# Retention's chunks in two groups, state tiles in pairs, and a table of later steps, in a one-layer hybrid decoder kernel

## The chip, the cores and the metric

The kernel runs on one core of a Trainium2 chip. The metric is the device time of one execution in microseconds (us); lower is better. The engines are TensorE (PE), VectorE (DVE), ScalarE (ACT), GpSimd (POOL) and SyncE (SP, which here only issues DMAs).

## The reference

One layer is computed for 520 tokens: a prompt of 512 and 8 single tokens of a decode step, width 1024, all in float32. The layer is a first half-step feed-forward, a token mixer of retention and gated delta rule side by side, and a second half-step feed-forward, each between two RMS norms.

```python
def layer(x, pos, s_ret, s_gdn, s_conv, ...):
    x = x + 0.5 * rmsnorm(swiglu(rmsnorm(x, ffn1_pre_g), ...), ffn1_post_g)
    m, s_ret_new, s_gdn_new, s_conv_new = token_mixer(rmsnorm(x, mix_pre_g), pos, ...)
    x = x + rmsnorm(m, mix_post_g)
    x = x + 0.5 * rmsnorm(swiglu(rmsnorm(x, ffn2_pre_g), ...), ffn2_post_g)

def step(s, inp):            # retention, one chunk
    q_, k_, v_, G_ = inp
    o = jnp.exp(G_)[..., None] * jnp.einsum('bhid,bhde->bhie', q_, s)
    gl = G_[..., -1:]
    s = jnp.exp(gl)[..., None] * s + jnp.einsum('bhjd,bhje->bhde', k_ * jnp.exp(gl - G_)[..., None], v_)
    return s, o              # plus (q k^T * decay) v inside the chunk
```

Retention and gated delta have 4 heads each, with states of 128 x 128; the decode tokens carry 8 states per head in from memory and the new states are outputs.

## The kernel before

The 520 tokens are two halves of 260 columns. A product in float32 is made as three passes: each weight tile is split into a rounded part whi (ACT, line 318) and the remainder wlo (DVE, line 319), each activation tile into a pair likewise (xhl, lines 477 and 478), and lines 380, 381 and 382 multiply high by high, low by high and high by low. These 128 x 128 by 260-column matmuls are "the stream"; the program has 8892 of them in a fixed order: first feed-forward (gate and up products g and u, some of them as seven products sv in place of eight, then down products dn), the mixer's input projections p, the branch products br and the output product, then the second feed-forward. Weights come by DMA from SP's queue (raw, line 246) and POOL's (line 266).

All other work is side work. It is written as Python generators ("tasks"), which `spawn` puts on a list. After about every six matmuls of the stream the program calls `tick`, which advances each task that is due; a task that yields n is due again n ticks later. So the order in which the instructions stand on each engine is fixed when the program is written, and each engine takes its own in that order. `spawn` looks up a table LATER by the task's name and how often it was spawned: at entry 0 its start is moved by so many ticks, at entry k the k-th yield that is not zero is made longer (or, with a negative number, shorter). Before the change, LATER is empty.

The side work that matters here:

- The norms ahead of a part (`pre_rms`): ACT squares the eight tiles of x by halves (line 495, sq), DVE adds them up in seven additions (line 509), PE sums over partitions with a matmul by ones (line 443, ss, one column per token group), DVE makes ms (line 433), POOL takes the reciprocal root rs (line 437), and PE spreads it over the partitions (line 449, rb). ACT and DVE copy rb out of PSUM (lines 531 and 529); products made before then are multiplied by it late. The norms behind a part (`post`) do the same with sums acc that DVE gathers (line 489).
- The gated delta heads (`gdn_head`): causal convolution (cv), its transposes (tr, line 1127), gates (gc and gbc, lines 1184 and 1206), sums of squares gsq summed by cs (line 1568), and an inverse in small blocks that travel through memory on SP's queue (lines 1480 and 1483).
- The retention heads (`ret_head`): for each of four chunks of 128 tokens PE writes the output (po, lines 1303 and 1304) and the chunk's addition to the state (line 1305) into one bank, DVE brings the state st forward (lines 1311 and 1307), ACT copies the output out (line 1312), DVE takes its mean and variance (lines 1314 and 1315).
- The decode states (`state_products`): eight tiles sd of four states each per kind, loaded by SP (line 1612) one ahead of its use; PE multiplies four states by 1 or 2 columns each (sp, line 1625), DVE copies the result out (line 1626).

Of the functions that are called but not changed, `tick` is this:

```python
    def tick(self):
        self.now += 1
        self.add_sums()
        self.prefetch()
        for t in list(self.tasks):
            if t[0] <= self.now:
                ...
                    steps = next(t[1])
                    if steps:
                        t[3] += 1
                        steps += t[2].get(t[3], 0)
                    t[0] = self.now + max(steps, 1)
```

Of the kernel before, what the change touches and what calls it, by code (L numbers as in the profile page):

```python
# [15 lines left out]
P = 128  # L16
# [24 lines left out]
SLOTS = 68  # L41
PLAIN = {1: 3, 2: 4}
# [3 lines left out]
LATER = {  # L46
}
# [82 lines left out]
class Kernel:  # L130
# [368 lines left out]
    def pre_rms(self, xs, r, plus):  # L499

        nc = self.nc
        self.sq = sq = [self.slot("sq") for _ in range(KD)]
        for hf in range(2):
            for k in range(KD):
                while len(xs[hf]) <= k:
                    yield 0
                self.square(k, hf, nc.scalar)
        for k in range(1, KD):
            nc.vector.tensor_tensor(sq[0], sq[0], sq[k], ALU.add)
        while not self.leads:  # L510
            yield 0
        yield 1
        yield from self.inverse_rms(sq[0], r, plus)
# [761 lines left out]
    def ret_head(self, h, q, k, v):  # L1275
# [23 lines left out]
        mv = self.const("mv", [P, NCH, 2])  # L1299
        for i in range(NCH):  # L1300
            po = self.bank("po")
            if i:
                nc.tensor.matmul(po[:, 0:P], qg[:, i, :], st[:, i - 1, :], start=True, stop=False)
            nc.tensor.matmul(po[:, 0:P], sT[:, i, :], vt[:, i, :], start=i == 0, stop=True)
            nc.tensor.matmul(po[:, P : 2 * P], kd[:, i, :], vt[:, i, :], start=True, stop=True)
            if i:
                nc.vector.scalar_tensor_tensor(
                    out=st[:, i, :], in0=st[:, i - 1, :], scalar=float(gamma**P), in1=po[:, P : 2 * P], op0=ALU.mult, op1=ALU.add
                )
            else:  # L1310
                nc.vector.tensor_copy(st[:, 0, :], po[:, P : 2 * P])
            nc.scalar.copy(po_sb[:, i, :], po[:, 0:P])
            bs = self.small("bs", [P, 6])
            nc.vector.bn_stats(bs, po[:, 0:P])
            nc.vector.bn_aggr(mv[:, i, :], bs)
            yield 3
# [298 lines left out]
    def state_products(self, src, rhs, n):  # L1615
# [3 lines left out]
        nxt = self.load_state(src, 0)  # L1619
        yield 10  # L1620
        for i in range(8):
            s, nxt = nxt, self.load_state(src, i + 1) if i < 7 else None
            ps = self.bank("sp")
            for b in range(4):
                nc.tensor.matmul(ps[:, b * n : (b + 1) * n], s[:, b, :], rhs(i // 2, 4 * (i % 2) + b), start=True, stop=True)
            nc.vector.tensor_copy(acc[:, i * 4 * n : (i + 1) * 4 * n], ps[:, 0 : 4 * n])
            yield 7
# [205 lines left out]
```

## Time and profile before

| what | value |
|---|---|
| median of 3 runs | 1244.01 us |
| lowest and highest | 1237.38 and 1244.2 us |
| the profiled execution | 1238.32 us, of which the span from first to last instruction is 1236.6 us |
| TensorE busy | 1197.2 us, 97% of the span |
| VectorE, ScalarE, GpSimd busy | 902.7, 576.2, 280.5 us |
| mean granted TensorE clock | 0.985 of full |

All durations below come from the one profiled execution. Busy time of PE counts the modelled ends of matmuls that overlap, so it says when PE had work, not that it ran at its peak; what was lost is read from idle time and from the granted clock. A releaser is inferred from the last semaphore event, and may name a neighbour of the true one.

### The profile page before, as it was taken

What the parts mean: (1) busy time and instruction counts of PE and PEld (TensorE: products, weight loads), DVE (VectorE), ACT (ScalarE), POOL (GpSimd) and SP (SyncE); (2) the same over time, 40 slices, a digit from 0 to 9 for tenths busy, and PEclk for the clock granted to TensorE, in tenths of its full rate; (3) what the DMA queues carried; (4) which work ended last, traced back from release to release, by engine and by line L of the source; (5) the groups of instructions that cost most, each with busy time, mean ns of one, the idle gap of its engine ahead of it and who ended that gap; (6) DMA issues with size and microseconds to landing.
All of it is one profiled execution on the core that took longest, in us unless ns stands there. A gap on an engine that the chain in (4) does not pass through costs nothing.

```text
span 1236.6 us, 25500 instructions
## 1 busy us (share of the span) xinstructions
PE 1197.2 (97%) x9921; PEld 1184.5 (96%) x9921; DVE 902.7 (73%) x1940; ACT 576.2 (47%) x1209; POOL 280.5 (23%) x501
## 2 busy tenths in 40 slices
PE   8999999999998999989999999999999999999995
PEld 8999999999997999989999999999999999999995
DVE  8988888676547788667666765546888888867554
ACT  6655666454334564312333243334565666653330
POOL 4211211000014248544443111212411111000003
PEclk9999999999998999999999999999999999999997
DMA  6787776223352433332343554442587777332352
GB/s 196 207 203 196 181 179 154 63 80 94 96 174 78 132 104 110 99 108 74 111 143 115 184 187 150 136 156 69 151 252 182 181 185 184 96 92 79 95 166 69
DMA packets 79689, 170.38 MB, mean 138 GB/s; under 512 B 17232, under 2 KB 20144, under 8 KB 79568
## 3 DMA queue, kind: packets, MB, share of 16 engines
q1 hardware_dynamic: 67280, 144.46, 36.6%
q0 software_dynamic: 12288, 24.29, 11.6%
q8 instruction: 78, 1.28, 0.4%
q14 instruction: 43, 0.35, 0.1%
HBM read 156.88 MB, written 11.83 MB: 136 GB/s over the span
## 4 chain that ended last, share of the span: by engine, by line
PE 73%; DVE 13%; ACT 5%; DMA 3%; issue 3%; POOL 2%; SPq 1%; DVEq 0%; ACTq 0%; POOLq 0%
PE sv L381 10%; PE sv L380 10%; PE sv L382 10%; PE p L380 5%; PE p L382 5%; PE p L381 5%; PE dn L380 5%; PE dn L382 5%; PE dn L381 5%; DVE wlo L319 3%; DVE cv L1242 2%; DMA raw<-dn_in 1%; PE br L380 1%; PE br L381 1%; PE br L382 1%
## 5 line engine op out<-in xcount | busy, mean ns | idle before, releaser
L380 PE MATMUL p<-xhl,whi 128*128 128x260 f32 x768 | 229.9, 299 | 0.0
L382 PE MATMUL p<-xhl,wlo 128*128 128x260 f32 x768 | 220.4, 287 | 0.2 <-DVE wlo L319 0.2
L381 PE MATMUL p<-xhl,whi 128*128 128x260 f32 x768 | 220.0, 286 | 0.0
L319 DVE TENSOR_TENSOR wlo<-raw,whi 128x1024 fp32r<-128x1024 f32 (+2 forms) x120 | 140.4, 1177 | 41.9 <-ACT whi L318 40.2
L381 PE MATMUL sv<-tl,w 128*128 128x260 f32 x592 | 167.5, 283 | 0.0
L380 PE MATMUL sv<-th,w 128*128 128x260 f32 x592 | 167.3, 283 | 0.0
L382 PE MATMUL sv<-th,w 128*128 128x260 f32 x592 | 166.9, 282 | 0.0
L380 PEld LDWEIGHTS p<-xhl,whi 128*128 128x128 f32 x768 | 148.4, 193 | 1.1
L381 PEld LDWEIGHTS p<-xhl,whi 128*128 128x128 f32 x768 | 148.4, 193 | 0.0
L382 PEld LDWEIGHTS p<-xhl,wlo 128*128 128x128 f32 x768 | 147.8, 192 | 0.4 <-DVE wlo L319 0.4
L337 DVE TENSOR_TENSOR w<-s,w 128x512 fp32r<-128x512 f32 x148 | 101.7, 689 | 39.6 <-ACT w L336 38.2
L266 POOL DMA_DIRECT2D s<-gu_in x74 | 65.3, 994 | 285.6 <-DMA s<-gu_in 138.2
L382 PE MATMUL dn<-hh,wlo 128*128 128x260 f32 x448 | 126.7, 283 | 1.2 <-DVE wlo L319 1.2
L380 PE MATMUL dn<-hh,whi 128*128 128x260 f32 x448 | 127.1, 284 | 0.0
L318 ACT CAST whi<-raw 128x1024 fp32r<-128x1024 f32 (+2 forms) x120 | 115.3, 970 | 24.8 <-DMA raw<-dn_in 16.4
L381 PE MATMUL dn<-hl,whi 128*128 128x260 f32 x448 | 126.3, 282 | 0.0
L382 PE MATMUL sv<-xhl,w 128*128 128x260 f32 x444 | 125.7, 283 | 0.0
L381 PE MATMUL sv<-xhl,w 128*128 128x260 f32 x444 | 125.5, 283 | 0.0
L380 PE MATMUL sv<-xhl,w 128*128 128x260 f32 x444 | 125.5, 283 | 0.0
L382 PEld LDWEIGHTS sv<-th,w 128*128 128x128 f32 x592 | 111.7, 189 | 0.0
L381 PEld LDWEIGHTS sv<-tl,w 128*128 128x128 f32 x592 | 111.5, 188 | 0.0
L380 PEld LDWEIGHTS sv<-th,w 128*128 128x128 f32 x592 | 111.4, 188 | 0.0
(412 smaller groups left out, 3266.6 us busy)
## 6 DMA issues: line engine op xcount, KB each, us to landing
raw<-gu_in SPq DMA_DIRECT2D x50, 512.0 KB, 5.0
raw<-win_in SPq DMA_DIRECT2D x48, 512.0 KB, 3.6
s<-gu_in SPq DMA_DIRECT2D x74, 256.0 KB, 5.5
s<-gu_in POOLq DMA_DIRECT2D x74, 256.0 KB, 5.4
raw<-dn_in SPq DMA_DIRECT2D x32, 448.0 KB, 3.4
a<-gu_in SPq DMA_DIRECT2D x37, 256.0 KB, 5.6
x<-x SPq DMA_DIRECT2D x32, 260.0 KB, 5.3
raw<-dn_in SPq DMA_DIRECT2D x16, 512.0 KB, 3.7
```

Source lines behind the costliest of these rows:

```text
L266: self.nc.gpsimd.dma_start(out=out, in_=term, accum_op=ALU.add)
L318: self.nc.scalar.copy(hi[:, ks], t[:, ks])
L319: self.nc.vector.tensor_tensor(lo[:, ks], t[:, ks], hi[:, ks].bitcast(F32), ALU.subtract)
L337: nc.vector.tensor_tensor(w[:, 1], t[i], w[:, 0].bitcast(F32), ALU.subtract)
L380: mm(ps, hi[:, k, :], xh, start=first, stop=False, skip_group_check=more)
L381: mm(ps, hi[:, k, :], xl, start=False, stop=False, skip_group_check=more)
L382: mm(ps, lo[:, k, :], xh, start=False, stop=last, skip_group_check=more)
L1242: nc.vector.scalar_tensor_tensor(out=acc, in0=cin[:, j : j + SEQ], scalar=w[:, j : j + 1], in1=acc, op0=ALU.mult, op1=ALU.add)
```

## The change

Four functions and the table change; the mathematics does not.

- `ret_head`: the four additions to the state come first, into one bank pu, and DVE makes all four states from it; after RET_WAIT = 5 ticks the seven output matmuls go into one bank po; one copy by ACT takes the whole bank, four pairs on DVE take mean and variance. The yields of 3 behind each chunk go; one of 3 is left.
- `state_products`: two state tiles are loaded at a time, eight matmuls go into one bank, one copy by DVE takes them. The first wait is 12 ticks in place of 10, the later ones are 14 in place of 7 for one tile.
- `pre_rms`: the sums of squares wait 4 ticks in place of 1 behind the condition that the part has started.
- LATER gets 41 entries. The program has only two `pre_rms` and four `gdn_head` tasks (the count starts at 0), so the entries for higher numbers move nothing.

```diff
--- before.py
+++ after.py
@@ -39,11 +39,53 @@
 RAW_BUFS, SPLIT_BUFS, AHEAD = 2, 9, 2
 SUM_LAG = 6
 SLOTS = 68
+RET_WAIT = 5
 PLAIN = {1: 3, 2: 4}
 SPLIT_H = (8, 21)
 
 
 LATER = {
...
+    ("gdn_head", 0): {0: 3},
...
+    ("post", 1): {0: 3, 1: -3, 3: -3, 9: 2},
...
+    ("pre_rms", 0): {0: 10},
+    ("pre_rms", 1): {0: 3, 1: 4},
...
 }
 
 
@@ -509,7 +551,7 @@
             nc.vector.tensor_tensor(sq[0], sq[0], sq[k], ALU.add)
         while not self.leads:
             yield 0
-        yield 1
+        yield 4
         yield from self.inverse_rms(sq[0], r, plus)
 
     def inverse_rms(self, acc, r, plus):
@@ -1297,23 +1339,28 @@
         st = self.slot("st", (P, NCH, P))
         po_sb = self.slot("ro", (P, NCH, P))
         mv = self.const("mv", [P, NCH, 2])
+
+        ps = self.bank("pu")
         for i in range(NCH):
-            po = self.bank("po")
+            nc.tensor.matmul(ps[:, i * P : (i + 1) * P], kd[:, i, :], vt[:, i, :], start=True, stop=True)
+        nc.vector.tensor_copy(st[:, 0, :], ps[:, 0:P])
+        for i in range(1, NCH):
+            nc.vector.scalar_tensor_tensor(
+                out=st[:, i, :], in0=st[:, i - 1, :], scalar=float(gamma**P), in1=ps[:, i * P : (i + 1) * P], op0=ALU.mult, op1=ALU.add
+            )
+        yield RET_WAIT
+        po = self.bank("po")
+        for i in range(NCH):
+            ci = slice(i * P, (i + 1) * P)
             if i:
-                nc.tensor.matmul(po[:, 0:P], qg[:, i, :], st[:, i - 1, :], start=True, stop=False)
-            nc.tensor.matmul(po[:, 0:P], sT[:, i, :], vt[:, i, :], start=i == 0, stop=True)
-            nc.tensor.matmul(po[:, P : 2 * P], kd[:, i, :], vt[:, i, :], start=True, stop=True)
-            if i:
-                nc.vector.scalar_tensor_tensor(
-                    out=st[:, i, :], in0=st[:, i - 1, :], scalar=float(gamma**P), in1=po[:, P : 2 * P], op0=ALU.mult, op1=ALU.add
-                )
-            else:
-                nc.vector.tensor_copy(st[:, 0, :], po[:, P : 2 * P])
-            nc.scalar.copy(po_sb[:, i, :], po[:, 0:P])
+                nc.tensor.matmul(po[:, ci], qg[:, i, :], st[:, i - 1, :], start=True, stop=False)
+            nc.tensor.matmul(po[:, ci], sT[:, i, :], vt[:, i, :], start=i == 0, stop=True)
+        nc.scalar.copy(po_sb, po.rearrange("p (c i) -> p c i", i=P))
+        for i in range(NCH):
             bs = self.small("bs", [P, 6])
-            nc.vector.bn_stats(bs, po[:, 0:P])
+            nc.vector.bn_stats(bs, po[:, i * P : (i + 1) * P])
             nc.vector.bn_aggr(mv[:, i, :], bs)
-            yield 3
+        yield 3
         nc.gpsimd.dma_start(out=self.a["sretp"][h], in_=st[:, NCH - 1, :])
         var = self.small("var", [P, NCH])
         nc.vector.tensor_scalar(var, mv[:, :, 1], EPS, None, ALU.add)
@@ -1616,15 +1663,16 @@
 
         nc = self.nc
         acc = self.cpool.tile([P, 32 * n], F32, name=self.name("sp"))
-        nxt = self.load_state(src, 0)
-        yield 10
-        for i in range(8):
-            s, nxt = nxt, self.load_state(src, i + 1) if i < 7 else None
+        load = lambda h: [self.load_state(src, i) for i in (2 * h, 2 * h + 1)]
+        nxt = load(0)
+        yield 12
+        for h in range(H):
+            s, nxt = nxt, load(h + 1) if h < H - 1 else None
             ps = self.bank("sp")
-            for b in range(4):
-                nc.tensor.matmul(ps[:, b * n : (b + 1) * n], s[:, b, :], rhs(i // 2, 4 * (i % 2) + b), start=True, stop=True)
-            nc.vector.tensor_copy(acc[:, i * 4 * n : (i + 1) * 4 * n], ps[:, 0 : 4 * n])
-            yield 7
+            for b in range(DEC):
+                nc.tensor.matmul(ps[:, b * n : (b + 1) * n], s[b // 4][:, b % 4, :], rhs(h, b), start=True, stop=True)
+            nc.vector.tensor_copy(acc[:, h * DEC * n : (h + 1) * DEC * n], ps[:, 0 : DEC * n])
+            yield 14
         self.prod = acc
 
     def decode_ret(self):
```

Up to the change in `ret_head`, line numbers of after are 42 above those of before. The order excerpts that follow are of the two programs.

The first place is SP's queue while the second gated delta head's inverse goes through memory (lines 1480 and 1483 before, 1527 and 1530 after); sd are the decode state tiles. Before:

```order
L1460 DMA L_7218<-s_1211_7212 128x1x512
L1612 DMA sd_7286<-sgdn_in 128x512
L246 DMA raw_7310<-win_in 128x1024
L1480 DMA s_1237_7347<-pack_6483 64x1x32 x8
L1483 DMA pack_6483<-s_1237_7347 32x4x32 x4
L1612 DMA sd_7400<-sgdn_in 128x512
L246 DMA raw_7431<-win_in 128x1024
L1612 DMA sd_7505<-sgdn_in 128x512
```

After:

```order
L1659 DMA sd_7210<-sgdn_in 128x512
L1659 DMA sd_7212<-sgdn_in 128x512
L288 DMA raw_7303<-win_in 128x1024
L1527 DMA s_1233_7341<-pack_6467 64x1x32 x8
L1530 DMA pack_6467<-s_1233_7341 32x4x32 x4
L288 DMA raw_7420<-win_in 128x1024
L1659 DMA sd_7430<-sgdn_in 128x512
L1659 DMA sd_7432<-sgdn_in 128x512
```

The tile that stood behind the eight transfers of line 1480 and the four of line 1483 now stands ahead of them, beside its neighbour; the pair that now stands behind them is the fourth.

The second place is ACT at the lead-in of the mixer, where x of the first half (x_4728 to x_4731) is scaled into xhl and squared into sq. Before, the end of the first half and the start of the second:

```order
L477 ACTIVATE xhl_5079<-x_4731,vec 128x260
L495 ACTIVATE sq_4976<-x_4731 128x260
L477 ACTIVATE xhl_5096<-x_4731,vec 128x260
L495 ACTIVATE sq_4977<-x_4731 128x260
L318 CAST whi_5105<-raw_4829 128x1024
L318 CAST whi_5111<-raw_4848 128x1024
L477 ACTIVATE xhl_5145<-x_4732,vec 128x260
L700 COPY early_5046<-p_5048 16x260
L700 COPY early_5046<-p_5051 128x260
L495 ACTIVATE sq_4970<-x_4732 128x260
```

After:

```order
L519 ACTIVATE xhl_5062<-x_4730,vec 128x260
L519 ACTIVATE xhl_5070<-x_4731,vec 128x260
L519 ACTIVATE xhl_5086<-x_4731,vec 128x260
L360 CAST whi_5094<-raw_4829 128x1024
L360 CAST whi_5100<-raw_4848 128x1024
L537 ACTIVATE sq_5106<-x_4728 128x260
L537 ACTIVATE sq_5107<-x_4728 128x260
L537 ACTIVATE sq_5108<-x_4729 128x260
L537 ACTIVATE sq_5109<-x_4729 128x260
L537 ACTIVATE sq_5110<-x_4730 128x260
L537 ACTIVATE sq_5111<-x_4730 128x260
L537 ACTIVATE sq_5112<-x_4731 128x260
```

The squares of the first half stood between the xhl operations; now the last two xhl operations of that half stand with the two casts behind them, and its eight squares in one block follow the casts.

The third place is DVE in the second retention head, around the copy that starts the state st; rp is the rotated query or key, wlo a split weight, bs and mv belong to mean and variance, AT to the inverse. Before:

```order
L1260 TENSOR_TENSOR u_7300<-p_7165,sin_5524 64x260
L1261 TENSOR_TENSOR rp_7294<-rp_7294,u_7300 128x260
L319 TENSOR_TENSOR wlo_7307<-raw_7007,whi_7306 128x1024
L1311 COPY st_7322<-po_7325 128x128
L1314 BN_STATS bs_7330<-po_7325 128x6
L1315 BN_AGGR mv_7324<-bs_7330 128x2
L1307 SCALAR_TENSOR_TENSOR st_7322<-st_7322,po_7370 128x128
L1314 BN_STATS bs_7376<-po_7370 128x6
L1315 BN_AGGR mv_7324<-bs_7376 128x2
L1415 TENSOR_SCALAR AT_5805<-pu_7397,cols_5702 128x128
```

After:

```order
L1302 TENSOR_TENSOR u_7293<-p_7164,sin_5523 64x260
L1303 TENSOR_TENSOR rp_7287<-rp_7287,u_7293 128x260
L361 TENSOR_TENSOR wlo_7300<-raw_7019,whi_7299 128x1024
L1346 COPY st_7315<-pu_7318 128x128
L1348 SCALAR_TENSOR_TENSOR st_7315<-st_7315,pu_7318 128x128 x3
L1361 BN_STATS bs_7385<-po_7376 128x6
L1362 BN_AGGR mv_7317<-bs_7385 128x2
L1361 BN_STATS bs_7388<-po_7376 128x6
```

The copy into st stands behind the same wlo, but the three steps that bring st forward now follow it at once (written as one row, x3), where before each had its own matmuls of po, mean and variance ahead of it.

## Rows read from the trace of the kernel before

**Rows 1.** The page's head and its first part: busy us (share of the span) xinstructions.

```profile
PE 1197.2 (97%) x9921; PEld 1184.5 (96%) x9921; DVE 902.7 (73%) x1940; ACT 576.2 (47%) x1209; POOL 280.5 (23%) x501
```

**Rows 2.** Windows: stretch, length, busy us (instructions) by engine, PE clock, DMA share, GB/s.

```profile
360.00:380.00 20.00, 16.68 (x138) 15.21 (x137) 13.58 (x27) 9.79 (x21) 9.22 (x11) 1.00 0.22 60
380.00:400.00 20.00, 17.55 (x128) 16.92 (x126) 13.87 (x24) 9.23 (x22) 8.34 (x9) 0.83 0.25 80
440.00:460.00 20.00, 20.00 (x169) 20.00 (x168) 16.80 (x42) 12.42 (x32) 8.95 (x18) 1.00 0.37 99
520.00:540.00 20.00, 20.00 (x172) 20.00 (x173) 15.04 (x45) 4.90 (x11) 10.37 (x28) 1.00 0.31 102
540.00:560.00 20.00, 16.76 (x129) 16.41 (x128) 8.86 (x27) 4.00 (x9) 7.24 (x18) 0.91 0.37 111
620.00:640.00 20.00, 19.51 (x174) 19.02 (x175) 13.62 (x38) 6.45 (x14) 12.26 (x38) 0.91 0.40 124
```

**Rows 3.** Waits of PE: line, what released it, total us, times, longest us.

```profile
PE ss L443 <- DVE acc L489: 4.5, 4, 1.8
PE ss L443 <- DVE sq L509: 2.9, 2, 2.5
PE cs L1568 <- DVE gsq L1680: 2.8, 1, 2.8
PE rb L449 <- POOL rs L437: 2.4, 2, 1.3
...
PE po L1303 <- POOL pack L1474: 1.6, 1, 1.6
PE sp L1625 <- DMA sd<-sgdn_in: 1.6, 1, 1.6
PE sp L1625 <- DMA sd<-sret_in: 1.2, 1, 1.2
...
PE tr L1127 <- ACT cv L1250: 1.0, 1, 1.0
PE ss L443 <- DVE sq L952: 0.7, 1, 0.7
```

**Rows 4.** Timeline of PE, mixer lead-in: start, length, operation, [idle before <-releaser].

```profile
362.67 0.62 PE L443 MATMUL ss<-ones,acc 128*87 128x1 f32 x6 [1.18 <-DVE acc L489]
...
393.06 1.92 PE L443 MATMUL ss<-ones,sq 128*87 128x1 f32 x12 [2.45 <-DVE sq L509]
...
399.92 1.24 PE L449 MATMUL rb<-cst,rs 87*128 87x87 f32 x10
```

**Rows 5.** Timeline of POOL, the same stretch.

```profile
395.25 2.25 POOL L437 TENSOR_TENSOR rs<-ms,mhalf 87x6 f32<-87x6 f32 x1 [8.40 <-DVE ms L433]
```

**Rows 6.** Timeline of PE, two stretches with small matmuls.

```profile
426.15 1.44 PE L1206 MATMUL gbc<-cst,gg 128*128 128x128 f32 x8
...
427.60 0.42 PE L381 MATMUL p<-xhl,whi 128*128 128x260 f32 x1
427.82 0.42 PE L382 MATMUL p<-xhl,wlo 128*128 128x260 f32 x1
...
519.49 0.95 PE L1625 MATMUL sp<-gkq,sd 128*128 128x2 f32 x8
520.30 0.47 PE L1303 MATMUL po<-st,rp 128*128 128x128 f32 x2
```

**Rows 7.** Timeline of SP's DMA queue while the second retention head runs.

```profile
543.27 5.87 SPq L1480 DMA_DIRECT2D s<-pack  x8
...
552.31 0.43 SPq L1612 DMA_DIRECT2D sd<-sgdn_in  x1
```

**Rows 8.** Timeline of DVE: second retention head; then lead-in of the second feed-forward.

```profile
542.08 0.28 DVE L1311 COPY st<-po 128x128 f32<-128x128 f32 x1
...
883.72 0.16 DVE L433 TENSOR_SCALAR ms<-ss 87x6 f32<-87x6 f32 x1 [1.18 <-PE ss L443]
...
891.22 0.42 DVE L529 COPY rb<-rb 128x260 f32<-128x260 f32 x1
```

More of the change, by code (lines that the diff above doesn't have):

```diff
@@ L46 @@
 LATER = {
+    ("begin", 0): {1: 1},
+    ("decode_gdn", 0): {10: 3},
+    ("down_operands", 0): {9: -3},
+    ("down_operands", 1): {5: -1},
+    ("finish_head", 1): {3: 1},
+    ("finish_head", 2): {1: 2},
+    ("finish_head", 3): {2: -1},
+    ("finish_head", 6): {2: 1},
+    ("finish_head", 7): {2: -1},
+    ("first", 12): {1: 7},
+    ("first", 30): {1: 2},
+    ("first", 4): {1: 2},
+    ("gdn_head", 0): {0: 3},
+    ("gdn_head", 1): {0: 3, 51: 1, 52: -3},
+    ("gdn_head", 2): {0: 3, 33: 5, 44: -5, 49: 2},
+    ("gdn_head", 3): {0: 3},
+    ("gdn_head", 4): {0: 3},
+    ("gdn_head", 5): {0: 3},
+    ("gdn_head", 6): {0: 3},
+    ("gdn_head", 7): {0: 3},
+    ("leads", 0): {1: 2},
+    ("leads", 1): {0: 3},
+    ("post", 0): {1: 2, 2: -1},
+    ("post", 1): {0: 3, 1: -3, 3: -3, 9: 2},
+    ("post", 3): {0: 2, 1: -7, 2: 1},
+    ("post", 4): {9: 2},
+    ("pre_rms", 0): {0: 10},
+    ("pre_rms", 1): {0: 3, 1: 4},
+    ("pre_rms", 2): {0: -1, 1: 3},
+    ("pre_rms", 3): {0: -1, 1: 3},
+    ("pre_rms", 4): {0: -1, 1: 3},
+    ("pre_rms", 5): {0: -1, 1: 3},
+    ("pre_rms", 6): {0: -1, 1: 3},
+    ("pre_rms", 7): {0: -1, 1: 3},
+    ("second", 12): {3: 3},
+    ("second", 16): {3: 5},
+    ("second", 23): {1: -5, 3: 3},
+    ("second", 32): {0: 3},
+    ("silu_later", 2): {0: -1, 1: 8},
+    ("silu_later", 3): {0: -3},
+    ("token_factors", 0): {0: -1, 6: -5},
 }
```

## The prediction

> **What bounds the kernel now.** I read the top of the page first: TensorE (PE) is busy 1197.2 us, 97% of the span [rows 1], so only 39 us of the span's 1236.6 are not matmul time, and the change removes no matmul of the large stream. What it can win is idle time of PE and time at the lower clock. The windows of 20 us come next [rows 2]: an undisturbed window (440 to 460) starts 169 matmuls, one each 20/169 = 0.118 us, at full clock. Where time was lost, PE is busy for less (16.68 at the least) or the granted clock is below 1.00. A mean of 0.91 over 20 us is 0.09 x 20 / 0.5 = 3.6 us at the lower level (half, 1.2 GHz); there two matmuls start 427.82 - 427.60 = 0.22 us apart [rows 6], so such a stretch loses 3.6 x (1 - 0.118/0.22) = about 1.6 us. The window with 0.83 holds nearly two, 3.1 us. The third view is PE's waits by releaser [rows 3]: nine entries there make 18.7 us of idle time. The reader should see that they have different causes: sums of squares that wait for VectorE (DVE) additions, a reciprocal root on GpSimd (POOL), and decode state tiles that come late from the queue of SyncE (SP). The trace lists no engine that PE follows throughout; each place has to be judged by itself.
>
> The side work is placed by ticks, one after about six matmuls of the stream, 6 x 0.118 = 0.7 us. I counted in the two programs before which matmul of the stream each side operation stands; "12 later" below means 12 matmuls, 1.4 us.
>
> **The change, part by part.** Gains are positive.
>
> *Start.* The sums of the first norm stand 6 matmuls later (0.71 us); they waited 0.7 us for line 952 [rows 3]. The whole of the rest of the program follows, PE being busy: +0.6.
>
> *Lead-in of the mixer, 360 to 402.* Here lie two of the four waits of ss on acc (one of 1.18 [rows 4]), rb on rs (1.3 of the 2.4) and ss on sq (2.5) [rows 3], and both lower stretches of the 0.83 window. They are not to be added. All the early waits lie ahead of one chain, which runs over the new x, its squares, seven additions on DVE, and the sums at 393.06 [rows 4]; a PE that waits less before it only arrives earlier and waits there. So I take the chain as fixed and ask what PE has done by 393.06. The sums now stand 18 matmuls later, and rb 12 later. Before, rb began at 399.92 with 12 matmuls fewer behind it, so the same place of the stream is at 399.92 + 12 x 0.118 = 401.3. After: sums at 393.06, half of their 1.92 us if the clock stays up, so to 394.0; rs is there 395.25 + 2.25 - (393.06 + 1.92) = 2.52 us after the sums' end [rows 4, 5], so 396.5, while 18 matmuls take 2.1, a new wait of 0.4. That is +4.8. If the clock falls all the same, 3.1 of this is lost: +1.7. Against it stands the move on ScalarE (ACT): eight squares that stood between the operations making xhl now come in one block ahead of the second half's xhl, and could hold up the chain itself. At 9.79/21 us each in the window 360 to 380 [rows 2] they make 3.7 us of ACT time; ACT is idle half of that window, and part of them only changes places with the casts, so I charge 0 to 1.0. For it, the additions of acc stand ahead of a t/xhl pair on DVE, which may start the chain earlier by as much as that 1.18. I take +3.0, ends +0.7 and +6.0.
>
> *The conv heads.* tr waits 1.0 for cv [rows 3] and stands 12 later: +1.0 (0 to 1.0; cv's own chain doesn't move). The column sum cs on gsq (2.8 us, the longest single wait [rows 3]) stands where it stood: 0, and nothing in the diff feeds it earlier.
>
> *Fewer, longer blocks.* Side matmuls interrupt the stream. Eight passes of sp at 519.49 delay the next block to 520.30, 0.81 us, though they last 0.95: the end of a block is covered by what follows [rows 6]. Eight more passes, spaced as the stream is, would add 0.95, so a block of sixteen costs 0.14 more than two of eight with their two ends covered. The state products go from sixteen blocks to eight, each retention head from four to two: sixteen merges, between 0 and -16 x 0.14 = -2.2. I take the middle, -1.1. DVE's eight and ACT's twelve copies that fall away are worth nothing: both are idle a quarter of the time or more, and the copies stand behind blocks that nobody waits for.
>
> *Retention's second head.* po waited 1.6 us [rows 3]; the profile names pack, but the operand is st, and the copy into st ran on DVE from 542.08 to 542.36, behind a wlo [rows 8]; ended by it, the wait began near 540.8. Afterwards po stands 30 matmuls, 3.5 us, behind the kd products in place of 18, so PE comes 12 x 0.118 = 1.4 us later, about 542.2. The first product needs no st; the copy and the three steps behind it on DVE, at its 0.28 us each, end at about 543.2. Left over is a wait of up to 0.8. So +0.8, ends 0 and +1.6. PSUM's banks: pu is held over the pause; the same number of banks is asked for by fewer takers, cost taken as nothing.
>
> *State tiles in pairs.* sp on sgdn_in waited 1.6, sp on sret_in 1.2 [rows 3]. The cause stands on SP's queue: the load of the tile was issued at 552.31, behind eight transfers of line 1480 that held the queue from 543.27 for 5.87 us, and four of line 1483 [rows 7]. In pairs, the third pair stands ahead of line 1480 (the first order excerpt of the change), and is needed 30 matmuls, 3.5 us, earlier than this tile was, but is issued over 9 us earlier; the fourth pair, behind it, is needed 54 matmuls later than the tile that waited, 6.4 us. Both waits go. After each wait the clock fell (windows 540 to 560 and 620 to 640 at 0.91 [rows 2]); without idle time ahead I expect it to stay. So 1.6 + 1.6 + 1.2 + 1.6 = +6.0; 2.8 if the clock falls anyway. One more SP issue ahead of line 1480 delays the packs of the inverse by about one issue, 0.43 us [rows 7]: nobody on PE waits for these in rows 3 now, so 0.
>
> Here **a rule of the Trainium skill** speaks against that clock term: "TensorE: Matmul & The Clock Gate" (section "Why this matters for your kernels") names idle gaps between bursts of matmuls, longer than any of these two, as what lowers the clock. By it these short waits were not the cause, and the two stretches here and the two of the lead-in would stay; the sum would be 6.3 lower. The rows disagree with it so far as both windows with such a wait have a lower clock, and the sum goes by them.
>
> *Decode finish.* Decode retention's last column sums come 12 matmuls later; what follows of them to the branch products passes through DVE's queue, which is what I expect to set their time still: 0, at the worst -1.4.
>
> *Second feed-forward.* The first sums wait 2.9 - 2.5 = 0.4 for sq [rows 3]; they stand 42 later, so that goes. But the factor rb comes 42 matmuls, 5 us, later too, 18 matmuls ahead of the product u, whose banks rb still holds. DVE copies rb out (line 529) at 891.22, 7.5 us after ms at 883.72, behind the operands of the sevens [rows 8]; from sums to u there are now 24 + 18 matmuls, 5.0 us, and up to 1.24 for rb itself [rows 4]. 7.5 - 6.2 = 1.3 of new wait: -0.9 in all, ends +0.4 and, if all of the 5 us shows, -4. The sums behind ffn1's second pass (ss on acc, the longest 1.8 [rows 3]) stand unchanged: 0.
>
> **Sum.** 0.6 + 3.0 + 1.0 - 1.1 + 0.8 + 6.0 - 0.9 = 9.4 us. On the profiled execution (1238.3, of which 1236.6 are the span) that is 1228.9. The three timed runs before lie at 1237.4, 1244.0 and 1244.2, the profiled one with the fastest; nothing in the one trace says what makes the other level. I take the changed kernel to be drawn from both levels, so I subtract from the middle of 1238.3 and 1244.0, 1241.2: **1232**, 1.0% under the median.
>
> **Rivals.**
> 1. *The waits move.* DVE's and POOL's chains set the lead-in and the second feed-forward's start, not PE's order, and the sums placed later only postpone r: the lead-in's low end 0.7 and -4 at u, conv heads 0. The sum is then 0.6 + 0.7 + 0 - 1.1 + 0.8 + 6.0 - 4 = 3.0, time 1238. The same time comes out if the waits go and the four lower stretches stay at their places, as the small-column blocks there stay: 9.4 - 6.3 = 3.1; 0.06 of this rival's chance is that case. For it: DVE is busy 73% [rows 1] and 13.58 of 20 us in the lead-in [rows 2]. Against: PE's own idle time there is what rows 3 show.
> 2. *The clock, and slower than before.* Blocks of sixteen sp passes of one or two columns, and po blocks, pull the clock down by themselves. For: behind the 1.44 us of gbc at 426.15 the stream runs at 0.22 spacing with no idle time at all [rows 6]. Against: the sp block at 519.49 stands among others, and 520 to 540 has clock 1.00 [rows 2]. Each of eight sp and four po blocks would cost 1.6, 19 us in all, and the gain from stretches removed stays out too, 6.3: 9.4 - 6.3 - 19.2 = -16.1, time 1257. With half of them, 1248. It turns the gain into a loss from the second new stretch beside the old ones on (3.1 / 1.6).
> 3. *All of it goes.* The lead-in gives +6, blocks cost nothing, po gains 1.6, u waits for nothing (+0.4): 0.6 + 6 + 1 + 1.6 + 6 + 0.4 = 15.6, time 1226. For: rows 3 hold all these waits.
> 4. *The placement isn't what the table says*, since several entries name tasks that don't exist (heads and norms above 3 and 1): those move nothing; the others are in the order excerpts. No chance of its own.
>
> **How the numbers follow.** Forecast 0.45, rival 1 0.22, rival 2 0.09, rival 3 0.24. The range: below, rival 3 and a little for the lower level (1238.3 - 15.6 = 1223): 1224. Above, rival 1 on the upper level, 1244 - 3 = 1241, and the milder clock case begins at 1244: 1243. Changes within 1% of 1244.0 (1231.6 to 1256.5) are about what a measurement of this kernel can't tell from no change. Rival 3 and 0.11 of the forecast lie below: faster 0.35. Slower by over 1% is only the full clock case: 0.03. Same 0.62.
>
> **What would show it.** In the changed trace: no wait of ss on sq in the mixer above 1 us and no half-clock stretch near 395; no waits of sp on sd, and windows 540 to 560 and 620 to 640 at 1.00; cs still 2.8 with its stretch; a new wait of u on a bank in the second feed-forward. New windows at 0.91 between 500 and 660 would be rival 2. I am wrong if PE's busy time, not its idle time, is what grows, or if the early part of the lead-in starts its chain later.

## The result, and the profile after

The changed kernel takes 1228.38 us (median of 4 runs, 1225.88 to 1229.19) against 1241.08 us for the kernel before (now 4 runs, 1237.38 to 1244.2). The ratio is 0.9895, with a 95% interval of 0.9862 to 0.9928: faster by 1.05%, 12.7 us between the medians. The forecast was 1232 us, in a range of 1224 to 1243. The span of the profiled execution fell from 1236.6 to 1227.4, by 9.2 us; the sum said 9.4 on this scale. These are one execution of each kernel, of the changed one the slowest of its four, of the one before one near its lowest; between the medians the gain is some 3 us above the sum. Below it is shown that the sum came out for partly wrong reasons.

The head and the first part of the changed kernel's page, to be held against [rows 1]:

```profile
span 1227.4 us, 25453 instructions
...
PE 1192.2 (97%) x9921; PEld 1179.4 (96%) x9921; DVE 898.7 (73%) x1932; ACT 575.0 (47%) x1197; POOL 278.4 (23%) x501
```

Its windows of 20 us, columns as in [rows 2]. Since the kernel runs ahead, the same work stands up to 12 us earlier than there:

```profile
360.00:380.00 20.00, 18.69 (x132) 16.92 (x131) 14.56 (x29) 11.05 (x26) 10.79 (x13) 0.83 0.30 78
380.00:400.00 20.00, 19.67 (x169) 19.04 (x169) 14.66 (x30) 8.53 (x20) 6.94 (x7) 1.00 0.21 72
480.00:500.00 20.00, 14.27 (x101) 13.84 (x100) 11.84 (x35) 2.84 (x4) 12.70 (x29) 0.83 0.38 97
540.00:560.00 20.00, 20.00 (x185) 19.84 (x183) 12.46 (x37) 6.72 (x14) 10.07 (x27) 1.00 0.40 116
560.00:580.00 20.00, 20.00 (x173) 19.44 (x172) 15.19 (x47) 3.15 (x8) 9.72 (x26) 0.91 0.23 62
620.00:640.00 20.00, 19.98 (x197) 19.19 (x196) 14.19 (x38) 7.76 (x20) 9.64 (x28) 1.00 0.37 123
```

PE's waits in the changed kernel, columns as in [rows 3]; line numbers are those of after (42 or 47 higher up to the state products):

```profile
PE cs L1615 <- DVE gsq L1728: 5.7, 1, 5.7
...
PE ss L485 <- DVE acc L531: 2.7, 2, 1.8
...
PE rb L491 <- POOL rs L479: 1.9, 3, 1.3
PE p L424 <- DVE wlo L361: 1.4, 1, 1.4
...
PE u L422 <- ACT rb L573: 0.6, 1, 0.6
PE sv L422 <- ACT q L848: 0.5, 1, 0.5
PE u L422 <- DVE h L832: 0.5, 1, 0.5
...
PE u L422 <- DVE rb L571: 0.3, 1, 0.3
```

What went is plain: of the nine entries in [rows 3], the waits of po on st, of sp on either kind of state tile, of tr on cv and of ss on sq are gone. What stayed is ss on acc (1.8, where nothing was moved) and rb on rs. What is new is 1.4 or shorter, and one old wait has grown: cs, 2.8 before, waits 5.7. The window 480 to 500 is the worst between the program's two ends now, 14.27 us busy at a clock of 0.83.

To see where the time came from I compared when the same matmul of the stream starts in the two profiled executions. The n-th matmul of the stream is the same product in both. The table gives the lead of the changed kernel; the last column is a second profiled execution of it (after_again, below).

| place (matmul of the stream) | lead, us | step, us | step in after_again, us |
|---|---|---|---|
| first feed-forward, to 2844 | 0.7 | +0.7 | -0.2 |
| mixer's lead-in, to 3060 | 5.0 | +4.3 | +5.4 |
| conv heads, to 3300 | 6.6 | +1.6 | 0.0 |
| to 3630 | 6.7 | +0.1 | +0.1 |
| cs, to 3720 | 3.1 | -3.6 | -1.3 |
| retention, gated delta, states, to 4560 | 10.1 | +6.9 | +6.8 |
| branch and output products, to 6100 | 11.7 | +1.7 | +0.7 |
| second feed-forward's start, to 6500 | 9.3 | -2.4 | -2.4 |
| rest, to the last | 9.3 | -0.1 | -0.5 |

The order of instructions is the same in the two executions. The steps of the lead-in, of the conv heads and of the branch products differ where a half-clock stretch stands in one of them only (near 373, 423 and 853); at cs the length of the wait differs too.

### The profile page after: what moved, and what is told of

The parts are those of the page before. It is cut to its first block, busy times and chain, and to the rows that moved or that the text cites. A ratio compares the mean times of both kernels' runs of the same rounds, so it can differ in the third digit from the quotient of the medians.

```text
span 1227.4 us, 25453 instructions
## 1 busy us (share of the span) xinstructions
PE 1192.2 (97%) x9921; PEld 1179.4 (96%) x9921; DVE 898.7 (73%) x1932; ACT 575.0 (47%) x1197; POOL 278.4 (23%) x501
## 4 chain that ended last, share of the span: by engine, by line
PE 79%; DVE 9%; ACT 4%; POOL 2%; issue 2%; DMA 2%; SPq 0%; ACTq 0%; DVEq 0%; POOLq 0%
PE sv L423 10%; PE sv L422 10%; PE sv L424 10%; PE p L422 6%; PE dn L422 6%; PE dn L424 6%; PE dn L423 6%; PE p L423 6%; PE p L424 6%; DVE wlo L361 2%; PE br L422 1%; PE br L423 1%; PE br L424 1%; PE g L423 1%; PE g L424 1%
## 5 line engine op out<-in xcount | busy, mean ns | idle before, releaser
L422 PEld LDWEIGHTS p<-xhl,whi 128*128 128x128 f32 x768 | 146.7, 191 | 1.0
L423 PEld LDWEIGHTS p<-xhl,whi 128*128 128x128 f32 x768 | 147.0, 191 | 0.0
```

The costliest lines, as they stand in the source:

```text
L422: mm(ps, hi[:, k, :], xh, start=first, stop=False, skip_group_check=more)
L423: mm(ps, hi[:, k, :], xl, start=False, stop=False, skip_group_check=more)
```

## The experiments

There were twelve runs, one of them of the changed kernel again. Ratios are to the kernel before on the same chip, with the 95% interval.

### The parts alone

The change is in three functions and the table. It is taken apart into `ret_head`, `state_products`, and the table with the longer pause in `pre_rms`.

**pairs_alone** is the kernel before with the new `state_products` only (the diff is in the part on the change).

> The kernel before with only the state products changed (two state tiles loaded and eight matmuls made per step). Sum of terms: both waits on state tiles (1.6 and 1.2) and the two half-clock stretches behind them (1.6 each) go, eight merges cost 0.1 each or less, so 5.2 to 6.0 us less, about 0.995 of before; windows 540 to 560 and 620 to 640 at clock 1.00. Rival, the clock depends on small-column blocks: the waits go but a stretch comes back behind a block of sixteen, 1.6 to 3.2 us of it lost: 2.5 to 4 us less.

Measured: 0.9977 (0.9960 to 0.9995), 2.9 us, half of the term of 6.0 (the medians, 1236.61 and 1237.96 us, are 1.4 apart). Waits of PE, two windows, and PE's timeline at two places:

```profile
PE po L1303 <- POOL pack L1474: 2.5, 2, 1.9
```

```profile
540.00:560.00 20.00, 18.09 (x143) 17.99 (x142) 10.38 (x30) 4.00 (x9) 7.24 (x18) 0.91 0.35 105
560.00:580.00 20.00, 20.00 (x181) 19.49 (x180) 14.90 (x45) 5.54 (x14) 10.09 (x29) 0.91 0.17 54
620.00:640.00 20.00, 19.77 (x194) 19.01 (x193) 15.24 (x39) 7.51 (x18) 13.35 (x36) 1.00 0.38 122
```

```profile
542.04 0.46 PE L1303 MATMUL po<-st,rp 128*128 128x128 f32 x2 [1.91 <-POOL pack L1474]
...
564.92 1.84 PE L1626 MATMUL sp<-gkq,sd 128*128 128x2 f32 x16
...
567.07 0.42 PE L382 MATMUL p<-xhl,wlo 128*128 128x260 f32 x1
```

No wait for a state tile is left, and the window 620 to 640 has its full clock. But two new entries stand against this. First, po waits 2.5 in two places: at the second head PE is 0.8 us earlier than before and DVE's copy into st, at 541.61, only 0.5. Second, two half-clock stretches are back between 540 and 580. The one at 567 follows a block of sixteen sp matmuls of two columns (1.84 us) with no idle time in it or ahead of it. The rival of the expectation holds: the waits go, part of the clock does not come back. In the trace 1.9 us are won between 3720 and 4560.

**ret_alone** is the kernel before with the new `ret_head` only (the diff is in the part on the change).

> The kernel before with only the retention heads changed (additions to the state first, outputs 5 ticks later). Sum of terms: the wait of the second head's po (1.6) falls by 0.8 to 1.6, eight merges cost up to 0.1 each: between 0.5 us slower and 1.0 faster, no difference in time. Rival, the longer blocks pull the clock down: one to four new half-clock stretches between 500 and 660 at 1.6 us each, up to 6 us slower.

Measured: 0.9978 (0.9958 to 0.9997), while the span of the profiled execution was 1236.7, that of before. The wait of po is gone, and one wait for a state tile is twice as long as before:

```profile
556.62 1.20 PE L1631 MATMUL sp<-gkq,sd 128*128 128x2 f32 x5 [3.28 <-DMA sd<-sgdn_in]
```

What was won at po (1.6) is given back at the state tile (1.6 before, 3.28 now), because the tile comes from SP's queue at its own time. The rival's new stretches don't show: one stands between 500 and 660, twice as long as those of before, which has two. Between 3720 and 4560 the trace gains 1.4 us. Alone, each of the two parts runs into the wait that the other one takes away, and in the whole change both waits are gone. No run has these two parts without the table, so it isn't shown how much of the 6.9 us there is theirs (see table_alone).

**norms_alone** is the kernel before with the later sums of squares ahead of the mixer and of the second feed-forward:

```diff
 LATER = {
+    ("pre_rms", 0): {0: 10},
+    ("pre_rms", 1): {0: 3, 1: 4},
 }
...
-        yield 1
+        yield 4
         yield from self.inverse_rms(sq[0], r, plus)
```

> The kernel before with only the later sums of squares ahead of the mixer and of the second feed-forward (the pause of 4 ticks and the two table entries of these norms). Sum of terms as the trace of the changed kernel shows them: about 4 us won at the mixer's lead-in, 1 to 1.5 us lost at the second feed-forward: 2.5 to 3 us less. Rival, given back: what is won ahead of the column sums cs of the decode step is lost there, since these wait for a series on GpSimd; the wait at cs grows from 2.8 to 4 us or more, and the time falls by 1 us or nothing.

Measured: 0.9988 (0.9965 to 1.0011), so no difference that shows. By the starts of the same matmuls, 4.0 us are won in the lead-in (lead 0.2 at 2844, 4.2 at 3060) and 2.4 lost at the second feed-forward (4.9 to 2.5 between 6100 and 6500). The lead isn't lost at cs (2.7, as before). 3.0 us of it go earlier, where the first conv heads' transposes now wait 2.4 for cv and a half-clock stretch follows (lead 4.2 at 3130, 1.2 at 3190; the stretch that before has at 427 isn't there, so it is 3.3 again at 3300):

```profile
413.15 0.66 PE L1129 MATMUL tr<-cst,cv 128*128 128x128 f32 x4 [2.42 <-ACT cv L1252]
```

Neither theory had this place: given back was right as a mechanism, cs was wrong as the place. In the whole change tr stands 12 later, and this wait is taken by the next.

**table_alone** is the kernel before with the whole table and the pause of 4; one entry is renumbered (the tenth yield of `decode_gdn` is its fourteenth with eight state steps).

```diff
-    ("decode_gdn", 0): {10: 3},
+    ("decode_gdn", 0): {14: 3},
```

> The kernel before with the whole table of later steps and the pause of 4 ticks, but retention heads and state products as before. If parts add up: the change's 9 us of span less the 5 to 6 of the state pairs and about 0 of the retention heads, so 3 to 4 us less than before, with the wait at cs at 5 to 6 us. Rival, the parts need each other: entries that were set for the new grouping make new waits in the old one, and the time is the same as before or longer.

Measured: 0.9936 (0.9912 to 0.9961), 7.9 us. The product of the three parts, 0.9936 x 0.9977 x 0.9978 = 0.9891, is the whole change's 0.9895 within the intervals. The table was worth more in time than I gave it (0.6 + 3.0 + 1.0 - 0.9 = 3.7), and cs waits 4.3 in its trace. Where the extra comes from is seen between 3720 and 4560: 3.7 us are won there, though the waits of po and sp are all but those of before:

```profile
PE po L1344 <- POOL pack L1515: 1.6, 1, 1.6
PE sp L1666 <- DMA sd<-sgdn_in: 1.5, 1, 1.5
```

```profile
540.00:560.00 20.00, 18.48 (x159) 18.30 (x158) 10.58 (x30) 3.73 (x8) 6.74 (x16) 1.00 0.30 90
```

The clock stays up: no half-clock stretch stands between 500 and 640, where the trace of before has two, one behind the same wait of sp (1.6 there) and one behind that of sp on sret_in (1.2 there, 0.7 here). So a wait of this length doesn't by itself bring a stretch. The three parts add up here, 1.9 (pairs) + 1.4 (retention) + 3.7 (table) = 7.0 us, as they do in time, against 6.8 to 6.9 in the whole change.

### The wait at cs, and the second feed-forward

Why cs waits longer is seen on DVE. gsq, which cs sums, stands behind five operations that make cols, and these wait for a root rr on POOL. DVE and POOL in the changed kernel, then rr in the kernel before:

```profile
484.87 0.16 DVE L1403 TENSOR_TENSOR cols<-se,rr 128x4 f32<-128x4 f32 x1 [2.30 <-POOL rr L1394]
...
487.81 0.23 DVE L1728 TENSOR_TENSOR gsq<-dcv 128x64 f32<-128x64 f32 x1 [0.35 <-ACT dcv L1725]
...
483.19 1.65 POOL L1394 TENSOR_TENSOR rr<-se,mhalf 128x8 f32<-128x8 f32 x1
```

```profile
486.86 1.65 POOL L1347 TENSOR_TENSOR rr<-se,mhalf 128x8 f32<-128x8 f32 x1
```

PE in the changed kernel:

```profile
488.09 0.37 PE L1615 MATMUL cs<-ones,gsq 128*64 128x1 f32 x2 [5.73 <-DVE gsq L1728]
...
488.99 0.42 PE L424 MATMUL p<-xhl,wlo 128*128 128x260 f32 x1
```

POOL runs a long series of small operations for the first head's inverse (pack) around rr. Between the two profiles of before and after, rr began 3.7 us earlier (483.19 against 486.86) where PE was 6.7 us earlier. So 3 us of PE's lead are lost at cs, and the stretch behind the wait is now two long.

The same sum can be made for every execution whose instructions stand in this order on PE, DVE and POOL up to here (three of them are variants described below). The wait is the 2.8 us of before and what rr falls short of PE's lead:

| execution | PE's lead at 3630, us | rr earlier by, us | 2.8 + difference | wait of cs, us |
|---|---|---|---|---|
| after | 6.7 | 3.7 | 5.8 | 5.7 |
| after_again | 5.3 | 3.9 | 4.2 | 4.2 |
| squares_spread | 6.6 | 5.3 | 4.1 | 4.0 |
| blocks_of_eight | 8.4 | 7.2 | 4.0 | 3.9 |
| ffn2_norm_back | 6.2 | 5.9 | 3.1 | 3.0 |

So the program doesn't fix the loss: one order of instructions loses 0.2 to 2.9 us here. What is the same in all five is DVE's own distance: gsq starts 6.47 us behind the start of the wlo that stands ahead of cols (5.95 before).

**gsq_early** moves the making of gsq three ticks forward and keeps cs where it is. On DVE it then stands ahead of cols; TensorE's order doesn't change.

```diff
-    ("decode_gdn", 0): {10: 3},
+    ("decode_gdn", 0): {1: -3, 2: 3, 10: 3},
```

> The changed kernel with the decode step's gsq made three ticks earlier, so that on VectorE it stands ahead of the five cols operations that wait for GpSimd's root rr; TensorE's order is the same. Given back, by the place in VectorE's queue: the wait of cs (5.7 us in the changed kernel) goes, and the two half-clock stretches behind it (3.1): up to 8 us less than the changed kernel. Given back, by GpSimd's series itself: cb, 30 matmuls behind cs, needs a root on GpSimd that stands behind the same series, so 4 to 5 us of the wait come up again at cb, and the time is 0 to 3 us under that of the changed kernel.

Measured: 0.9868 (0.9852 to 0.9884), median 1223.73 us. DVE and PE:

```profile
478.15 1.23 DVE L361 TENSOR_TENSOR wlo<-raw,whi 128x1024 fp32r<-128x1024 f32 x1
...
481.61 0.23 DVE L1728 TENSOR_TENSOR gsq<-dcv 128x64 f32<-128x64 f32 x1 [0.35 <-ACT dcv L1725]
481.75 0.16 DVE L1403 TENSOR_TENSOR cols<-se,rr 128x4 f32<-128x4 f32 x1
```

```profile
482.39 0.28 PE L1615 MATMUL cs<-ones,gsq 128*64 128x1 f32 x2
...
486.82 0.43 PE L1622 MATMUL cb<-cst,gdm 64*128 64x64 f32 x2
...
494.31 0.56 PE L1547 MATMUL pV<-pack,AT 32*32 32x32 f32 x16 [1.25 <-DVE pack L1537]
```

cs no longer waits, and neither does cb, 30 matmuls further on; cols follow gsq at 481.75 without a wait in between. The lead over the changed kernel's profile grows by 7.9 us from 3630 to 3660; 1.2 of it is given back at pV (1.25, waiting for the inverse's pack), the rest stays to the end. Of the 7.9, not all is the edit's. gsq now starts 481.61 - 478.15 = 3.46 us behind the start of that wlo in place of 6.47, so the place in DVE's queue was worth 3.0 us of wait, and a stretch of 1.6 where one goes with it. But DVE and POOL also stand 3.1 to 3.2 us earlier in this execution than in the changed kernel's profile, at the same lead of PE: this wlo at 478.15 against 481.34, rr at 480.07 against 483.19. That part belongs to the execution. In time, too, the price is open: by the ratios it is 3 to 5 us under the changed kernel, which was not measured beside it, while two variants on this run's own chip that keep gsq late (ffn2_norm_back and blocks_of_eight below, each with a gain of its own) are only 0.8 and 1.8 us slower.

**gsq_cb_later** adds 42 matmuls ahead of cs and cb:

```diff
+    ("decode_gdn", 0): {1: -3, 2: 10, 5: -7, 10: 3},
```

> As gsq_early, and cs and cb also 42 matmuls (5 us) later, with the state products where they were. By the place in the queues: neither cs nor cb waits, the half-clock stretches at 486 to 493 go, 4 to 8 us less than the changed kernel. By GpSimd's series: the next that needs it, pV of the first head's inverse, waits in their place for 3 us or more, and the gain over the changed kernel is under 3 us.

Measured: 0.9883 (0.9865 to 0.9900), so no more than gsq_early. pV waits 1.3 here too, and three half-clock stretches stand between 495 and 561 (gsq_early has one there). The first theory is right about the waits, and nothing is gained by going further.

**gsq_on_before** was meant to do the same to the kernel before.

```diff
 LATER = {
+    ("decode_gdn", 0): {1: -3, 2: 3},
 }
```

> The kernel before with only gsq moved ahead of the cols operations. If the wait at cs belongs to the place in VectorE's queue: its 2.8 us and the half-clock stretch behind it (1.6) go, 3 to 4.4 us less than before. If GpSimd's series holds this stretch together: the wait comes up at cb or pV, 1 us or less is won.

Measured: 1.0007 (0.9990 to 1.0024), cs waits 2.5. The edit failed to move gsq past cols, and VectorE has the order of before, as have TensorE and ScalarE. In the kernel before, cols stand three ticks earlier than in the changed one (`gdn_head` 3 starts 3 ticks later there), so three ticks don't bring gsq past them; only two fills of constants on POOL changed places. The run says nothing on the theory, but is a second run of before.

**ffn2_norm_back** puts the norm of the second feed-forward where it was:

```diff
-    ("pre_rms", 1): {0: 3, 1: 4},
+    ("pre_rms", 1): {1: -3},
```

> The changed kernel with the sums of squares of the second feed-forward where they stood before. If the later factor is what makes the waits there (u on rb 0.6 and 0.3, u on h 0.5, sv on q 0.5): these go, 0.4 for sq comes back, 1.5 us less than the changed kernel. If these waits come from PE being earlier by 10 us or from the operands of the sevens on VectorE: no difference.

Measured: 0.9878 (0.9859 to 0.9898), median 1224.49. Between 6100 and 6500 it wins 1.1 us over the changed kernel. u and sv no longer wait; ss on sq and g on h do:

```profile
PE cs L1615 <- DVE gsq L1728: 3.0, 1, 3.0
...
PE ss L485 <- DVE sq L551: 1.3, 2, 0.9
...
PE g L422 <- DVE h L832: 0.6, 1, 0.6
```

So the later factor cost 1.1 of the 2.4 us that are lost there. The other 1.3 were not tracked down. The rest of the 4 us between the medians isn't this edit's: in the profile 2.8 us were won ahead of 6100, where the program is the changed kernel's, most of it at cs, which waits 3.0 here.

**squares_spread** takes the first half's squares apart again on ACT:

```diff
-    ("pre_rms", 0): {0: 10},
+    ("pre_rms", 0): {},
```

> The changed kernel with the first half's eight squares of the mixer's norm back between the xhl operations on ScalarE; the sums on TensorE stay late. If the block of squares is what buys the lead-in: the wait of ss on sq or of p on xhl grows, 1 to 2 us more than the changed kernel. If the later place of the sums alone buys it: no difference of 1 us or more, the lead-in still 4 us shorter than before.

Measured: 0.9902 (0.9880 to 0.9925), the changed kernel's own time. Between 2844 and 3060 it wins 1.2 us on the first profile of the changed kernel, and after_again 1.1: the same. The block of squares on ACT neither buys nor costs anything; the later sums are what counts.

### The clock, and the end

**blocks_of_eight** keeps the loads in pairs, and multiplies in two blocks:

```diff
+            for j in range(2):
+                ps = self.bank("sp")
+                for b in range(4):
+                    nc.tensor.matmul(ps[:, b * n : (b + 1) * n], s[j][:, b, :], rhs(h, 4 * j + b), start=True, stop=True)
...
+                yield 7
```

> The changed kernel with state tiles still loaded in pairs, but multiplied in two blocks of eight matmuls 7 ticks apart, so twice as many and shorter blocks. If the longer blocks cost by themselves (0.09 each) or by the clock (the stretch at 561 stands behind a block of sixteen): 0.7 to 2.3 us less than the changed kernel. If the count of blocks decides: the same or up to 1 us more. In both, no wait for a state tile.

Measured: 0.9889 (0.9871 to 0.9907), median 1225.53; not told apart from the changed kernel by time. Its windows between 540 and 600:

```profile
540.00:560.00 20.00, 20.00 (x183) 19.84 (x183) 14.01 (x40) 5.30 (x12) 9.84 (x25) 1.00 0.29 89
560.00:580.00 20.00, 19.87 (x186) 19.27 (x185) 16.66 (x60) 4.85 (x9) 11.56 (x32) 1.00 0.26 84
580.00:600.00 20.00, 20.00 (x172) 19.68 (x171) 11.73 (x40) 7.12 (x13) 10.34 (x23) 1.00 0.43 120
```

No half-clock stretch there. All seven profiled executions of the change and its variants with blocks of sixteen (after, after_again, gsq_early, gsq_cb_later, gsq_and_norm, ffn2_norm_back, squares_spread) have one, within 0.7 us of the end of one of their eight blocks of sixteen: near 560 in six of them, at 590 in after_again. Between 3720 and 4560 the lead over the changed kernel's profile grows by 1.4 us, which is that one stretch. The count and length of the blocks as such cost nothing that shows. The length of a block is not the whole cause of a stretch: table_alone, the other execution with the table and blocks of eight, has none between 500 and 640 either, but most blocks of sixteen have no stretch behind them.

**after_again** is the changed kernel a second time.

> The changed kernel itself once more, on the same chip as its corrected forms: 0.9895 of before within 0.003. Its trace shows what differs between two executions of one program: if the double half-clock stretch near 375 and the wait of 5.7 us at cs belong to the program, both come again; if they depend on the execution, the stretches stand elsewhere and the wait at cs is 3 to 5 us.

Measured: 0.9908 (0.9883 to 0.9933), median 1228.32. The second expectation holds:

```profile
PE cs L1615 <- DVE gsq L1728: 4.2, 1, 4.2
```

```profile
360.00:380.00 20.00, 17.71 (x146) 15.91 (x145) 14.00 (x28) 10.84 (x24) 10.04 (x12) 1.00 0.30 81
420.00:440.00 20.00, 20.00 (x159) 19.98 (x159) 16.43 (x40) 15.92 (x52) 7.86 (x9) 0.91 0.38 130
480.00:500.00 20.00, 15.81 (x119) 15.21 (x119) 12.50 (x37) 3.54 (x6) 13.20 (x32) 0.91 0.36 98
580.00:600.00 20.00, 20.00 (x158) 19.68 (x157) 12.24 (x40) 5.54 (x11) 10.14 (x26) 0.91 0.40 118
```

The double stretch near 375 isn't there, one near 425 is, and cs waits 4.2 and not 5.7. So a term of "a stretch goes" holds for one execution only, where the block behind which it stood is still in the program.

**gsq_and_norm** puts gsq_early and ffn2_norm_back together.

> The changed kernel with both corrections: gsq ahead of the cols operations on VectorE, and the sums of squares of the second feed-forward where they were before. If the two places are independent, as their distance suggests: the gains add, 5 to 6 us by gsq and 1 to 1.5 by the norm, 6 to 7.5 us under the changed kernel, about 0.984 of before. If the gain at gsq is given back at waits further on: 2 to 4 us under the changed kernel.

Measured: 0.9858 (0.9832 to 0.9884), median 1221.01 (1220.76 to 1223.05) against 1228.32 (1225.2 to 1229.42) for the changed kernel on the same chip: 7.3 us less, as the first expectation has it. In the two profiles 4.5 us of it lie at cs and 1.2 between 6100 and 6500. It is the fastest of the kernels that ran.

```profile
480.00:500.00 20.00, 18.86 (x177) 18.11 (x176) 13.93 (x42) 6.26 (x12) 13.15 (x36) 1.00 0.49 146
540.00:560.00 20.00, 20.00 (x174) 19.72 (x173) 13.31 (x33) 5.29 (x12) 9.62 (x27) 0.91 0.28 87
```

The window 480 to 500, at 14.27 us and 0.83 in the changed kernel, is at 18.86 and full clock; a stretch remains at 555, behind a block of sixteen.

## Why the prediction was right, and where its steps were not

The time lies in the range, 4 us under the forecast, and the sign is right. The sum, 9.4 us, is met by the 9.2 of the two profiled spans and is some 3 short of the 12.7 between the medians (11.9 where after_again was measured). By its steps:

**Lead-in of the mixer**, +3.0 (ends 0.7 and 6.0): +4.3 and +5.4 in two executions. The argument from the chain held: ss on sq doesn't wait, and rb begins with the small new wait that the working gave it, 0.33 for rs where 0.4 stood:

```profile
392.63 1.02 PE L485 MATMUL ss<-ones,sq 128*87 128x1 f32 x12
...
396.23 0.56 PE L491 MATMUL rb<-cst,rs 87*128 87x87 f32 x3 [0.33 <-POOL rs L479]
```

The charge for the block of squares was needless (squares_spread).

**Conv heads**, +1.0: the step failed in after_again (0.0), and the +1.6 of the first execution is the stretch of [rows 6] at 427 that wasn't there, since the waits make up for each other. (In the other variants it is within 0.1 of 0, with a stretch near 421, and 1.5 in blocks_of_eight, without one.) What was late next was not named: a split weight, wlo, on DVE, for which p waits 1.4 (the waits above), as much as tr had waited for cv and more.

**cs**, 0: the step that failed most, at -3.6 and -1.3. I held that what stands unchanged costs nothing. But PE came 6.7 us earlier, and gsq only 3.7; the wait grew by the difference, from 2.8 to 5.7 (4.2 in the other execution), with stretches behind it. The size of the loss varies between executions: the three variants with the same order up to there lost 0.3 to 2.4. gsq_early shows that it needn't have stood: gsq comes 3.0 us earlier by its place alone.

**Blocks**, -1.1: about 0 (blocks_of_eight), but for the clock. **Retention's second head**, +0.8, and **state tiles**, +6.0: together with the blocks 5.7 foretold, 6.9 and 6.8 found. The two are not separate terms: alone they gained 1.9 and 1.4 us in the trace, since each ran into the other's wait, and the table brought 3.7 by itself, with the waits in place. Half of the +6.0 was clock, on the ground that a stretch comes from the wait ahead of it. That ground failed on both sides: table_alone has the waits and no stretch, and stretches also follow blocks of sixteen with no wait at all. So that 6.9 lies near 5.7 is in part luck. Three of the stretches between 500 and 640 in the trace of before and of pairs_alone stand behind waits, and in each execution of the change one stands behind such a block, at 1.6 us. The second rival named such blocks, and was wrong in its number, one stretch and not twelve.

The rule of the Trainium skill that was weighed there ("TensorE: Matmul & The Clock Gate", section "Why this matters for your kernels") named only long idle gaps. The runs bear it out no better: the clock fell behind short waits and, in the change, behind none, and it stayed up behind others of the same length (table_alone); which waits or blocks it follows differs between executions of one program.

**Second feed-forward**, -0.9 (ends +0.4 and -4): -2.4. The mechanism is shown in size 1.1 by ffn2_norm_back, and u waits on the copies of rb as foretold (0.6 and 0.3 for ACT's and DVE's copy); the term was mis-sized by another 1.3 that stays open.

**Start**, +0.6, and **decode finish**, 0: +0.7 and -0.2 by 2844, within what two executions differ; no wait at the decode's end but oh (1.1, as before). The +1.7 from 4560 to 6100 was not foretold at all: it is in the main the stretch at 864 of before, which the changed kernel's profile doesn't have and after_again has at 853.

So in the first profile the total came out because the lead-in, the conv heads, the middle and the branch products gave 4.9 us more than the sum had for them, in good part by stretches that stood elsewhere, and cs and the second feed-forward took 5.1 away. That these are equal is luck.

## What to carry to other kernels

An engine that is busy 97% of the time still follows others: a lead won at one place lasts until the next chain that has a start of its own, so the wait ahead of an unchanged place has to be costed with the new arrival time, and a part that shows little alone may only have moved PE on to the next wait. When a wait grows, look first at what stands ahead of the operand's maker on its own in-order engine: eight short operations moved ahead of five that waited for another engine took 3.0 us off the wait behind them here. One profile of each kernel doesn't price such an edit: the wait itself was 3.0 to 5.7 us in five executions of one order of instructions. Terms for the clock shouldn't be booked like terms for waits; two executions of one program differ by a stretch or two.

## What the runs showed of the hardware

Half-clock stretches follow blocks of small-column matmuls without idle time: 1.84 us of sixteen matmuls of one or two columns had one behind them once in each of seven executions, while blocks of eight, most of them 7 to 10 us apart, had none in blocks_of_eight and table_alone. A wait of sp of 1.6 us had one behind it in the trace of before, the same wait of 1.5 us none in that of table_alone. The stretches stand at different places in executions of the same program, and each costs about 1.6 us.

On POOL the small steps of pack took 0.2 to 0.3 us in most places of the changed kernel's profile and 0.5 to 1.3 in 23 of 252; in 13 of the 23, and in all eight over 1 us, DVE was at a wlo at the same time, which subtracts two operands in SBUF. One of them, DVE first:

```profile
481.34 1.23 DVE L361 TENSOR_TENSOR wlo<-raw,whi 128x1024 fp32r<-128x1024 f32 x1
...
481.57 1.08 POOL L1522 TENSOR_TENSOR pack<-pack 128x16 f32<-128x16 f32 x1
482.73 0.21 POOL L1521 TENSOR_TENSOR pack<-L,pack 128x12 f32<-128x12 f32 x1
```

The Trainium skill has this rule ("SBUF — State Buffer", section "Who interferes with whom"): an operation of DVE with two inputs in SBUF and one of GpSimd that reads SBUF take a port pair in turns, and the second waits for the whole of the first. The rows agree: 481.57 + 1.08 = 482.65 ends 0.08 us behind 481.34 + 1.23 = 482.57. Such waiting is a small part of why rr did not keep up with PE's lead in that profile: ahead of rr the slow steps took 8.2 us more than 0.24 each, against 7.7 in the trace of before. In ffn2_norm_back, where rr lost least, they took 6.2, but in blocks_of_eight, where it lost 1.2 us, 8.0: what else makes rr late stays open.
